# Convolution input product: channel blocks 2 to 6 by seven products, block 7 in full from tokens loaded a second time

## The chip, the cores and the metric

The kernel runs on one core of one Trainium2 chip. The metric is the device time of one execution in microseconds (us). The engines are TensorE (PE; its weight loads are PEld), VectorE (DVE), ScalarE (ACT), GpSimd (POOL) and SyncE (SP), which issues all of this kernel's transfers (DMA).

## What is computed

The reference is a decoder trunk of two layers in fp32, with 1024 tokens of 1024 channels. The first layer mixes tokens with a causal Conformer convolution, the second with sliding-window attention; each is followed by layer norm, an MLP with squared ReLU and a gated embedding. Only the convolution's start is touched here:

```python
def conformer_conv(x, w_in, b_in, w_dw, b_dw, ln_g, ln_b, w_out, b_out):
    h = x @ w_in + b_in                      # 1024 -> 2048
    a, gate = jnp.split(h, 2, axis=-1)
    h = a * jax.nn.sigmoid(gate)
    h = lax.conv_general_dilated(            # depthwise, 31 taps, causal
        h, w_dw[:, None, :], window_strides=(1,), padding=[(CONV_WIDTH - 1, 0)],
        dimension_numbers=("NWC", "WIO", "NWC"), feature_group_count=D_MODEL) + b_dw
    h = jax.nn.silu(layer_norm(h, ln_g, ln_b))
    return h @ w_out + b_out
```

## The kernel before

**Arithmetic.** Each fp32 operand is split into a high part and a remainder of a narrower type (fp32r): ScalarE casts (`xh`, `wh`), VectorE subtracts (`xl`, `wl`). A product is three matmuls, high by high, low by high and high by low (`mm3`, L663).

**Order.** The program is first recorded, and a list scheduler (`Recorder.schedule`, L318 to L454) then puts the instructions of all engines in an order, from a cost for each operation. For a DMA it takes the free time of the queue, and an amount that grows with the elements times partitions of the first operand (L446 to L449). Each engine runs its instructions in the order so made, and every instruction is recorded at line 466 (`issue`); so the profile's groups are told apart by tile names. `nc.later(n)` moves the due time of what is recorded under it, by `FORMS_BY` = 200 and `BACK_BY` = 300 for two parts of the convolution.

**Input products.** `conv` (L818 to L1129) works on eight channel blocks `c`; each has 128 channels of `a` and 128 of the gate, over two halves of 512 tokens. The tokens are held split as `xh`, `xl` in eight chunks of 128 input channels for each half. Blocks 0 to 2 (`c < ALONE`, `conv_in`) are computed in full: 2 outputs x 2 halves x 8 chunks x 3 = 96 matmuls of 128x512. Blocks 3 to 7 go by a Strassen-like scheme of seven products of half the depth (`conv_seven`): 7 x 4 x 3 = 84 matmuls. It needs differences of weight chunks (`pair_units`, L1224) and differences of token chunks, T1 to T4. `forms` (L854) makes T1 to T3: for each of four `k` it loads four token chunks from DRAM, three into `g` buffers (of which there are four) and one into an `E` buffer, takes the differences on VectorE, splits each into two buffers taken from other names (A, bo, v, B, X), and so frees the `g` buffers for the next `k`. `last_forms` (L871) splits T4 into the home of the tokens of the second half (`xT[0,1]`, tiles `xh`, `xl`), which so lose the plain tokens; it is called at the first block that goes by seven products.

**Exchange and taps.** `hand_over` (L836) splits a gated half (tile `zz`; `wh` for the last half of block 7) and stores it to DRAM (`scr`) in eight transfers. `taps` (L973) runs `LAG` = 6 steps behind: it loads `B` from `scr` with the tokens of a group on partitions, loads a band matrix `z` from `w_dw` (128x576, 288 KB; 64 of them in all), casts it into `E` on ScalarE over 128 partitions, puts the remainder of its upper 64 partitions beside it on VectorE, and does nine matmuls of 128x256 for each band, 72 for a block. The sums go to `g`, with the bias added by ScalarE, are transposed by TensorE (`tr<-ident,g`) and copied out: for blocks 0 to 6 (`c < KEPT`) as 128x512 to a `t` buffer and then to DRAM (`kept`). At block 7 the kept values come back into `X` and `A` in 64-element pieces, and block 7's own are copied beside them.

**After it.** `conv_ln` (L1053) is the layer norm: statistics on VectorE, scaling on POOL, transposes on TensorE, SiLU on ScalarE; `mix_out` is the output product. The embedding's products (`embed`, L1131; tiles `ps<-wh,wh`) need nothing from the convolution and are placed among the last taps and the layer norm.

Of the kernel before, what the change touches and what calls it, by code (L numbers as in the profile page):

```python
# [10 lines left out]
F32 = mybir.dt.float32  # L11
F32R = mybir.dt.float32r
# [3 lines left out]
P = 128  # L16
# [32 lines left out]
             ps=6, tr=2, sc=0, pv=0, mid=0)  # L49


ALONE = 3
KEPT = 7
FORMS_BY, BACK_BY = 200, 300
FORM_HOMES = ("A", 9), ("bo", 2), ("v", 1), ("B", 4), ("X", 8)
LATE = 100
# [66 lines left out]
class View:  # L123
# [30 lines left out]

    def to_broadcast(self, shape):
        return View(self.buf, np.broadcast_to(self.idx, shape[1:]), self.parts, self.steps + (("bro", shape),))

    def real(self):
        a = self.buf.tile
# [37 lines left out]
class Recorder:  # L197
# [120 lines left out]
    def schedule(self):  # L318
# [85 lines left out]
        while True:  # L404
            best = None
            for e in engs:
                while rdy[e] and rdy[e][0][2].end:
                    heapq.heappop(rdy[e])
                while fut[e] and fut[e][0][3].end:
                    heapq.heappop(fut[e])  # L410
                if rdy[e]:
                    t = free[e]
                elif fut[e]:
                    t = max(free[e], fut[e][0][0])
                else:
                    continue
                if best is None or t < best[0]:
                    best = (t, e)
            if best is None:
                break  # L420
            t, e = best
            while fut[e] and fut[e][0][0] <= t:
                r, p, i, o = heapq.heappop(fut[e])
                if not o.end:
                    heapq.heappush(rdy[e], (p, i, o))
            p, i, o = heapq.heappop(rdy[e])
            if WAIT and fut[e] and e != "tensor":
                r, p2, i2, o2 = fut[e][0]
                if not o2.end and r <= t + WAIT and p2 < p - 300:
                    heapq.heappush(rdy[e], (p, i, o))  # L430
                    heapq.heappop(fut[e])
                    t, o = r, o2
            if o.eng == "either":
                o.eng = e
                o.dur = self.cost(o, o.outv, o.allv)
            d = o.dur
            if e == "scalar" and o.name == "activation":
                k = TABLE.get(o.args[2].name if len(o.args) > 2 else "", 0)
                if k and k != table:
                    table = k  # L440
                    d += 1283.0
            if both(o):
                d += max(0.0, held["gpsimd" if e == "vector" else "vector"] - 50.0 - t)
                held[e] = t + d
            free[e] = t + d
            if e == "sync":  # L446
                v = o.allv[0]
                dma = max(dma, t + 1400.0) + v.n * v.parts / 75.0
                finish(o, max(dma, t + 2800.0))  # L449
            else:  # L450
                finish(o, t + d)
# [47 lines left out]
class Emit:  # L499
# [318 lines left out]
    def conv(self):  # L818
# [8 lines left out]
        ws.add(*[lambda k=k: self.prep(d["w_in"][0, k], range(4 * k, 4 * k + 4)) for k in range(2)])  # L827
        ws.pump()
        for c in range(1, 8):
            ws.add(*([d["w_in"][c, 0], d["w_in"][c, 1]] if c < ALONE else self.pair_units([d["w_in2"][c - ALONE, k] for k in range(2)])))  # L830
        nc.sync.dma_start(cc, d["cconst"])
        nc.sync.dma_start(self.ident, d["ident"])
        scr = {}
# [1 line left out]

        def hand_over(c, h, g):  # L836

            both = self.sb("wh" if (c, h) == (7, 0) else "zz", F32R, 2 * HT)
            self.split(g, both[:, 0:HT], both[:, HT : 2 * HT])
            for j in range(NG):  # L840
                if j % 2 == 0 and (c, j // 2) not in scr:
                    scr[c, j // 2] = nc.tile(f"scr{c}_{j // 2}", (P, 2 * U), F32, "DRAM")
                o = j % 2 * U + h * P
                cols = slice(o, o + P)
                dst = scr[c, j // 2].scatter(
                    lambda a, cols=cols: a.rearrange("(k p) u -> p k u", p=CG)[:, :, cols], CG, cols, 2 * PH
                )
                src = both.bitcast(F32)[j * CG : (j + 1) * CG, :].rearrange("p (k u) -> p k u", k=2 * PH)
                nc.sync.dma_start(dst, src)
# [84 lines left out]

        def conv_in(c):

            if c >= ALONE:
                yield from conv_seven(c)
                return
            us = ws.get(2)  # L940
            for h in (0, 1) if c == 0 else (1, 0):
                pp = [self.ps() for s in range(2)]

                def part(s, kb):
                    wh, wl = us[kb // 4]
                    o = (kb % 4) * 256 + (1 - s) * P
                    tr = [(wh[:, o : o + P], wl[:, o : o + P], *self.xs(kb, h * HT, HT))]
                    self.mm3(pp[s], tr, kb == 0, kb == KB - 1)

                if c == 0:  # L950
                    for kb in range(KB):
                        part(0, kb)
                        part(1, kb)
                    yield
                else:
                    for s in range(2):
                        for kb in range(KB):
                            part(s, kb)
                        if s == 0:
                            yield  # L960
                sg = self.sb("t")
                nc.scalar.activation(sg, pp[0], AF.Sigmoid, bias=bg[:, c : c + 1], scale=1.0)
                g = self.sb("t")
                nc.vector.scalar_tensor_tensor(
                    out=g, in0=pp[1], scalar=ba[:, c : c + 1], in1=sg, op0=ALU.add, op1=ALU.mult
                )
                hand_over(c, h, g)
                yield
            ws.done(2)
# [3 lines left out]
        def taps(c):  # L973
# [3 lines left out]
            for jj in range(2):  # L977
                pss = [self.ps() for k in range(2)]
                for j in range(2):
# [3 lines left out]
                    nc.sync.dma_start(G2[:, :, HIST : HIST + U], scr[c, 2 * jj + j].rearrange("p (k u) -> p k u", k=2))  # L983
                    exchange = nc.ops[-1]
                    for k in range(2):
                        w = nc.tile("z", (P, n))
                        nc.sync.dma_start(w, d["w_dw"][c, jj, 2 * j + k])
                        w = w.rearrange("p (m q) -> p m q", q=PH * CG)
                        e = bands[turn[0] % len(bands)]
                        turn[0] += 1  # L990
                        ev = e.rearrange("p (m o q) -> p m o q", o=2, q=PH * CG)
                        if e in fresh:
                            fresh.remove(e)
                            nc.gpsimd.memset(ev.bitcast(F32)[LOW, :, 1, :], 0.0)
                        nc.scalar.copy(ev[:, :, 0, :], w)
                        nc.vector.tensor_tensor(
                            out=ev[HIGH, :, 1, :], in0=w[HIGH], in1=ev[HIGH, :, 0, :].bitcast(F32), op=ALU.subtract
                        )
                        for i in range(SHIFTS):
                            o = k * LO + HIST - i  # L1000
                            nc.tensor.matmul(
                                pss[k][:, j * U : (j + 1) * U], e[:, i * P : (i + 1) * P], G[:, o : o + U],
                                start=i == 0, stop=i == SHIFTS - 1,
                            )
# [19 lines left out]
                        nc.tensor.transpose(pv[:, h, j], y[:, o : o + P], self.ident)  # L1024
                nc.slack = 0.0
                if c < KEPT:
                    s = self.sb("t")
                    (nc.scalar.copy if jj else nc.vector.tensor_copy)(s, pt)
                    nc.sync.dma_start(kept[:, (2 * c + jj) * HT : (2 * c + jj + 1) * HT], s)
                    yield  # L1030
                    continue
                if c == KEPT and jj == 0:
                    kv = kept.rearrange("p (c s u) -> p c s u", c=2 * KEPT, s=2 * PH)
                    for q in range(2):
                        m = min(8, 2 * KEPT - 8 * q)
                        for h in range(2):
                            for f in range(PH):
                                Z[h, f, q] = self.sb("XA"[q])
                                dst = Z[h, f, q][:, 0 : 64 * m].rearrange("p (c u) -> p c u", u=64)
                                with nc.later(BACK_BY):  # L1040
                                    nc.sync.dma_start(dst, kv[:, 8 * q : 8 * q + m, PH * h + f, :])
                for h in range(2):
                    for f in range(PH):
                        o = c % 4 * P + jj * 4 * CG
# [43 lines left out]
            forms()  # L1088
        more_bands()
        kept = self.dram("kept", 2 * KEPT * HT)  # L1090
        ins = (x for c in range(8) for x in conv_in(c))
        outs = (x for c in range(8) for x in taps(c))
        for n in range(32 + LAG):
# [902 lines left out]
def layout(a):  # L1996
# [12 lines left out]
    r["xT"] = c(x[phased].T.reshape(KB, P, T))  # L2009
    r["pT"] = c(np.stack([p[0][phased], p[1]]).transpose(0, 2, 1).reshape(2, 2, P, T))  # L2010
    wi = np.asarray(a["conv_w_in"])[0]
    r["w_in"] = c(wi.reshape(2, 4, P, 2, 8, P).transpose(4, 0, 2, 1, 3, 5).reshape(8, 2, P, 1024)[:ALONE])

    w2 = wi[:, np.concatenate([np.arange(D, 2 * D), np.arange(D)])].reshape(8, P, 2, 8, P)
    r["w_in2"] = c(w2.transpose(3, 2, 1, 0, 4).reshape(8, 2, P, 1024)[ALONE:])
# [12 lines left out]
    for q in range(CG):  # L2028
        band[:, :, :, :, q, :, q] = wt[:, :, :, :, q, :]
    band = band.reshape(8, 2, 4, P // 2, SHIFTS * PH * CG)  # L2030
    r["w_dw"] = c(np.concatenate([band, band], axis=3))

    bd = np.asarray(a["conv_b_dw"])[0].reshape(32, 2, CG).transpose(2, 1, 0).reshape(CG, 64)
    r["cconst"] = c(
# [45 lines left out]
```

## Time and profile before

| what | us |
|---|---|
| median of 3 runs | 2142.71 (2142.64 to 2142.78) |
| the profiled execution | 2142.3 |
| its span in the profile | 2140.5 |
| TensorE busy | 2116.5 |
| VectorE busy | 1757.5 |
| ScalarE busy | 1152.3 |
| GpSimd busy | 280.6 |

The convolution's input products and taps take about the first 260 us of the span, its layer norm and output product come after, the first MLP then runs to about 1000 us. A line of the page's groups reads "engine operation out<-in shape x count | busy us, mean ns | idle before, and what ended it"; a line of the timeline reads "start, duration, engine, operation, tiles, count [idle before it <- what ended it]". Matmuls overlap, so the mean duration of one (some 390 ns) is more than the distance from one to the next.

### The profile page before, as it was taken

Reading aid. Unit: us, or ns where it says so; the run is one execution under the profiler, and the core shown is the slowest. Engines: PE = TensorE matmul, PEld = TensorE weight load, DVE = VectorE, ACT = ScalarE, POOL = GpSimd, SP = SyncE. Lnnn points to the kernel's source line nnn. Section 1 sums busy time; section 2 is a strip of 40 time slices with the busy share of each in tenths; the row PEclk is TensorE's granted clock in tenths of the full one; section 3 lists DMA queues with packets and bytes.
Section 4 is the critical chain, followed back from the end, with each engine's and each line's share of the span. In section 5 each row is a group of like instructions: output and inputs, shape, how many; then the busy total and the mean of one; then the engine's idle time right before and its main releaser. Section 6 shows DMA issues by size and latency. Waiting matters only on the chain.

```text
span 2140.5 us, 29992 instructions
## 1 busy us (share of the span) xinstructions
PE 2116.5 (99%) x10008; PEld 1752.9 (82%) x10008; DVE 1757.5 (82%) x2854; ACT 1152.3 (54%) x2146; POOL 280.6 (13%) x495
## 2 busy tenths in 40 slices
PE   9999899999999999999999999999999999999999
PEld 7888778888888888888788888888888888888877
DVE  6866579988898788876986888689988988788688
ACT  5655554654544633335755888445445554333484
POOL 0000052200000000001320656240000000000042
PEclk9999999999999999999999999999999999999999
DMA  9877965867786756655487022665778795565726
GB/s 295 234 203 203 268 245 177 285 222 250 264 271 231 278 177 204 201 184 213 156 284 249 11 89 79 208 239 184 257 267 296 262 332 174 179 233 170 262 75 230
DMA packets 228939, 462.46 MB, mean 216 GB/s; under 512 B 38192, under 2 KB 64432, under 8 KB 228784
## 3 DMA queue, kind: packets, MB, share of 16 engines
q1 hardware_dynamic: 228784, 460.54, 65.1%
q8 instruction: 79, 1.29, 0.2%
q14 instruction: 76, 0.62, 0.1%
HBM read 312.34 MB, written 148.11 MB: 215 GB/s over the span
## 4 chain that ended last, share of the span: by engine, by line
PE 40%; DVE 5%; ACT 3%; DMA 2%; issue 1%; POOL 1%; SPq 0%; POOLq 0%; DVEq 0%; ACTq 0%
PE ps L466 31%; PE tr L466 9%; DVE xl L466 1%; DMA t<-proj 1%; ACT z L466 1%; DVE t L466 1%; POOL sm L466 1%; DVE z L466 1%; DVE sm L466 0%; DVE A L466 0%; DVE B L466 0%; ACT xh L466 0%; DMA raw<-in_w_kv_dram 0%; ACT t L466 0%; DMA raw<-gate_t 0%
## 5 line engine op out<-in xcount | busy, mean ns | idle before, releaser
L466 PE MATMUL ps<-xh,xl 128*128 128x512 f32 x636 | 247.6, 389 | 0.0
L466 PE MATMUL ps<-xh 128*128 128x512 f32 x636 | 247.6, 389 | 0.0
L466 PE MATMUL ps<-xl,xh 128*128 128x512 f32 x636 | 247.6, 389 | 0.0
L466 ACT CAST wh<-raw 128x1024 fp32r<-128x1024 f32 (+2 forms) x156 | 143.4, 923 | 134.7 <-PE ps L466 84.0
L466 POOL TENSOR_SCALAR sm<-sm 128x1 f32<-128x1 f32 x72 | 28.3, 397 | 1364.0 <-DVE E L466 612.0
L466 PE MATMUL ps<-xl,wh 128*128 128x512 f32 x508 | 198.7, 392 | 0.0
L466 PE MATMUL ps<-xh,wl 128*128 128x512 f32 x508 | 198.3, 391 | 0.0
L466 PE MATMUL ps<-xh,wh 128*128 128x512 f32 x508 | 196.1, 392 | 0.9 <-ACT xh L466 0.9
L466 PE MATMUL ps<-wh,xh 128*128 128x512 f32 (+1 forms) x404 | 159.2, 395 | 1.7 <-ACT zz L466 0.9
L466 PE MATMUL ps<-wh,xl 128*128 128x512 f32 (+1 forms) x404 | 160.4, 397 | 0.0
L466 PE MATMUL ps<-wl,xh 128*128 128x512 f32 (+1 forms) x404 | 159.3, 394 | 0.0
L466 ACT CAST wh<-g 128x512 fp32r<-128x512 f32 x128 | 76.4, 620 | 153.8 <-PE ps L466 73.7
L466 ACT CAST xh<-wh 128x1024 fp32r<-128x1024 f32 x76 | 79.7, 1049 | 118.0 <-PE tr L466 90.4
L466 PEld LDWEIGHTS ps<-xl,xh 128*128 128x128 f32 x636 | 119.4, 188 | 24.9
L466 PEld LDWEIGHTS ps<-xh,xl 128*128 128x128 f32 x636 | 119.4, 188 | 24.7
L466 PEld LDWEIGHTS ps<-xh 128*128 128x128 f32 x636 | 119.5, 188 | 24.6
L466 DVE TENSOR_TENSOR wl<-raw,wh 128x1024 fp32r<-128x1024 f32 (+1 forms) x100 | 100.0, 1001 | 35.5 <-ACT wh L466 35.1
L466 DVE TENSOR_TENSOR xl<-wh,xh 128x1024 fp32r<-128x1024 f32 x76 | 92.8, 1221 | 25.6 <-ACT xh L466 25.6
L466 PEld LDWEIGHTS ps<-xh,wh 128*128 128x128 f32 x508 | 95.4, 188 | 22.5 <-ACT xh L466 1.6
L466 PEld LDWEIGHTS ps<-xh,wl 128*128 128x128 f32 x508 | 95.5, 188 | 19.5
L466 PEld LDWEIGHTS ps<-xl,wh 128*128 128x128 f32 x508 | 95.4, 188 | 19.5 <-DVE xl L466 1.3
L466 DVE TENSOR_TENSOR wl<-g,wh 128x512 fp32r<-128x512 f32 x128 | 84.6, 686 | 26.8 <-ACT wh L466 26.8
(447 smaller groups left out, 5620.0 us busy)
## 6 DMA issues: line engine op xcount, KB each, us to landing
wh<-hid SPq DMA_DIRECT2D x78, 512.0 KB, 4.1
raw<-in_w_up_dram SPq DMA_DIRECT2D x61, 512.0 KB, 4.3
wl<-in_w_down_dram SPq DMA_DIRECT2D x58, 512.0 KB, 4.8
hid<-zz SPq DMA_DIRECT2D x96, 256.0 KB, 4.0
z<-in_w_dw_dram SPq DMA_DIRECT2D x64, 288.0 KB, 4.0
hid<-t SPq DMA_DIRECT2D x70, 256.0 KB, 3.0
raw<-hid SPq DMA_DIRECT2D x30, 512.0 KB, 3.7
B<-scr SPq DMA_DIRECT2D x32, 256.0 KB, 4.5
```

The source lines that it names most:

```text
L466: getattr(getattr(nc, o.eng), o.name)(*a, **k)
```

## The change

`ALONE` becomes 2, a new `LAST` is 7 and `KEPT` becomes 6. Blocks 2 to 6 go by seven products; blocks 0, 1 and 7 are computed in full. Since `last_forms` has overwritten the plain tokens of the second half's first four chunks, block 7 loads and splits these four chunks again, and starts with the half that has not been overwritten, and for the second half with the other four chunks. The number of matmuls stays at 10008.

Besides, the band matrices are loaded on 64 partitions (144 KB) and cast twice by ScalarE, once into each half of the partitions. The values kept in DRAM are ordered by half and phase, written in pieces of 128 elements and read back in one piece for each partition; block 6 is no longer kept but copied like block 7, which makes 16 more small copies. The scheduler's price of a DMA becomes the larger one of its operands' (9 ns for each contiguous piece and 0.0366 ns for each byte, over 16), which changes the order of instructions elsewhere too.

```diff
-ALONE = 3
-KEPT = 7
+ALONE = 2
+LAST = 7
+KEPT = 6
...
+    def transfer(self):
+
+        i = self.idx.ravel()
+        pieces = self.parts * (1 + int((np.diff(i) != 1).sum()))
+        return (9.0 * pieces + 0.0366 * 4 * i.size * self.parts) / 16
...
             if e == "sync":
-                v = o.allv[0]
-                dma = max(dma, t + 1400.0) + v.n * v.parts / 75.0
+                dma = max(dma, t + 1400.0) + max(v.transfer() for v in o.allv)
                 finish(o, max(dma, t + 2800.0))
...
-            ws.add(*([d["w_in"][c, 0], d["w_in"][c, 1]] if c < ALONE else self.pair_units([d["w_in2"][c - ALONE, k] for k in range(2)])))
+            ws.add(*([d["w_in"][c, 0], d["w_in"][c, 1]] if c < ALONE or c >= LAST else self.pair_units([d["w_in2"][c - ALONE, k] for k in range(2)])))
...
-            both = self.sb("wh" if (c, h) == (7, 0) else "zz", F32R, 2 * HT)
+            both = self.sb("wh" if (c, h) == (LAST, 1) else "zz", F32R, 2 * HT)
...
-            if c >= ALONE:
+            if ALONE <= c < LAST:
                 yield from conv_seven(c)
                 return
             us = ws.get(2)
-            for h in (0, 1) if c == 0 else (1, 0):
+            if c == LAST:
+                for kb in range(KB // 2):
+                    self.load_xT(1, kb)
+            for h in (0, 1) if c in (0, LAST) else (1, 0):
                 pp = [self.ps() for s in range(2)]
+                order = [(kb + KB // 2 * (h if c == LAST else 0)) % KB for kb in range(KB)]
...
-                        w = nc.tile("z", (P, n))
+                        w = nc.tile("z", (P // 2, n))
                         nc.sync.dma_start(w, d["w_dw"][c, jj, 2 * j + k])
...
-                        nc.scalar.copy(ev[:, :, 0, :], w)
+                        for rows in (HIGH, LOW):
+                            nc.scalar.copy(ev[rows, :, 0, :], w)
                         nc.vector.tensor_tensor(
-                            out=ev[HIGH, :, 1, :], in0=w[HIGH], in1=ev[HIGH, :, 0, :].bitcast(F32), op=ALU.subtract
+                            out=ev[HIGH, :, 1, :], in0=w, in1=ev[HIGH, :, 0, :].bitcast(F32), op=ALU.subtract
                         )
...
                 if c < KEPT:
-                    s = self.sb("t")
-                    (nc.scalar.copy if jj else nc.vector.tensor_copy)(s, pt)
-                    nc.sync.dma_start(kept[:, (2 * c + jj) * HT : (2 * c + jj + 1) * HT], s)
+                    for h in range(2):
+                        if jj == 0:
+                            wait[h] = self.sb("t")
+                        v = wait[h].rearrange("p (f j u) -> p f j u", f=PH, j=2)
+                        src = pt[:, h * 256 : (h + 1) * 256].rearrange("p (f u) -> p f u", f=PH)
+                        (nc.scalar.copy if h else nc.vector.tensor_copy)(v[:, :, jj, :], src)
+                        if jj:
+                            dst = kept.rearrange("p (s c u) -> p s c u", s=2 * PH, c=KEPT)
+                            nc.sync.dma_start(dst[:, PH * h : PH * h + PH, c, :], wait[h].rearrange("p (f u) -> p f u", f=PH))
                     yield
                     continue
                 if c == KEPT and jj == 0:
-                    kv = kept.rearrange("p (c s u) -> p c s u", c=2 * KEPT, s=2 * PH)
                     for q in range(2):
-                        m = min(8, 2 * KEPT - 8 * q)
+                        m = min(4, KEPT - 4 * q)
...
-                                    nc.sync.dma_start(dst, kv[:, 8 * q : 8 * q + m, PH * h + f, :])
+                                    nc.sync.dma_start(Z[h, f, q][:, 0 : P * m], kept[:, o : o + P * m])
...
+        wait = {}
```

More of the change, by code (lines that the diff above doesn't have):

```diff
@@ L947, in part @@
                     tr = [(wh[:, o : o + P], wl[:, o : o + P], *self.xs(kb, h * HT, HT))]
-                    self.mm3(pp[s], tr, kb == 0, kb == KB - 1)
+                    self.mm3(pp[s], tr, kb == order[0], kb == order[-1])
                 if c == 0:
@@ L956, in conv_in @@
                     for s in range(2):
-                        for kb in range(KB):
+                        for kb in order:
                             part(s, kb)
@@ L1038, in taps @@
                                 Z[h, f, q] = self.sb("XA"[q])
-                                dst = Z[h, f, q][:, 0 : 64 * m].rearrange("p (c u) -> p c u", u=64)
+                                o = ((PH * h + f) * KEPT + 4 * q) * P
                                 with nc.later(BACK_BY):
-                                    nc.sync.dma_start(dst, kv[:, 8 * q : 8 * q + m, PH * h + f, :])
+                                    nc.sync.dma_start(Z[h, f, q][:, 0 : P * m], kept[:, o : o + P * m])
                 for h in range(2):
@@ L2011, in layout @@
     wi = np.asarray(a["conv_w_in"])[0]
-    r["w_in"] = c(wi.reshape(2, 4, P, 2, 8, P).transpose(4, 0, 2, 1, 3, 5).reshape(8, 2, P, 1024)[:ALONE])
+    r["w_in"] = c(wi.reshape(2, 4, P, 2, 8, P).transpose(4, 0, 2, 1, 3, 5).reshape(8, 2, P, 1024))
     w2 = wi[:, np.concatenate([np.arange(D, 2 * D), np.arange(D)])].reshape(8, P, 2, 8, P)
@@ L2030, in layout @@
     band = band.reshape(8, 2, 4, P // 2, SHIFTS * PH * CG)
-    r["w_dw"] = c(np.concatenate([band, band], axis=3))
+    r["w_dw"] = c(band)
     bd = np.asarray(a["conv_b_dw"])[0].reshape(32, 2, CG).transpose(2, 1, 0).reshape(CG, 64)
```

## The prediction

> **What bounds the kernel now.** I read the page's busy shares first, then busy time by stretches, the waits of TensorE, its timeline around them, and last the queues that feed it. Of the page:
>
> ```profile
> span 2140.5 us, 29992 instructions
> PE 2116.5 (99%) x10008; PEld 1752.9 (82%) x10008; DVE 1757.5 (82%) x2854; ACT 1152.3 (54%) x2146; POOL 280.6 (13%) x495
> ```
>
> TensorE is the bound nearly everywhere, and the order of instructions shows 10008 matmuls in both kernels. So the change cannot remove matmul time; it can only remove or make idle time on TensorE. Where that is, the busy time by stretches shows (us, busy and count of PE, PEld, DVE, ACT, POOL, granted clock, DMA share, GB/s):
>
> ```profile
> 50.00:225.00 175.00, 174.43 (x997) 152.55 (x996) 125.67 (x188) 102.84 (x183) 4.75 (x31) 1.00 0.77 221
> 225.00:310.00 85.00, 76.20 (x423) 63.20 (x422) 56.74 (x108) 50.05 (x97) 27.83 (x33) 0.98 0.89 278
> 310.00:1000.00 690.00, 688.97 (x3067) 569.09 (x3066) 586.68 (x849) 320.08 (x480) 26.12 (x27) 1.00 0.69 230
> ```
>
> The steady convolution (50 to 225 us) loses 0.6 us and the first MLP 1.0 us; the end of the convolution with its layer norm (225 to 310 us) loses 8.8. That stretch is what can be won. What TensorE waits for in it (total us, times, longest), and where (start, duration, idle before in brackets):
>
> ```profile
> PE ps L466 <- DVE E L466: 2.1, 2, 1.1
> PE ps L466 <- POOL X L466: 1.8, 1, 1.8
> PE ps L466 <- DVE g L466: 1.7, 2, 1.2
> PE ps L466 <- ACT xh L466: 1.6, 1, 1.6
> PE tr L466 <- POOL X L466: 1.0, 3, 0.4
> PE ps L466 <- POOL A L466: 0.5, 1, 0.5
> ```
> ```profile
> 55.16 2.31 PE L466 MATMUL ps<-B,E 128*128 128x256 f32 x18
> ...
> 228.74 4.46 PE L466 MATMUL ps<-B,E 128*128 128x256 f32 x36
> 234.30 1.34 PE L466 MATMUL ps<-B,E 128*128 128x256 f32 x9 [1.09 <-DVE E L466]
> 236.67 2.12 PE L466 MATMUL ps<-B,E 128*128 128x256 f32 x9 [1.03 <-DVE E L466]
> ...
> 252.07 8.77 PE L466 MATMUL ps<-B,E 128*128 128x256 f32 x72
> 260.68 0.40 PE L466 MATMUL ps<-wh,wl 128*128 128x512 f32 x1
> ```
>
> The last input product ends at 228.74, the last tap at 260.68: 31.9 us. The 72 taps took 260.68 - 252.07 = 8.6 us, 0.12 each. A 128x512 matmul costs 0.227 (16.32 us for 72, in the chain of waits):
>
> ```profile
> 1502.43 16.32 PE ps L466 x72
> ```
> ```profile
> L466 PE MATMUL ps<-B,E 128*128 128x256 f32 x126 | 16.7, 292 | 2.1 <-DVE E L466 2.1
> L466 PE MATMUL ps<-wh,wh 128*128 128x512 f32 x12 | 5.0, 415 | 3.3 <-DVE g L466 1.7 <-ACT xh L466 1.6
> ```
>
> By these groups of the tail (228.7 to 260.8), it holds 126 taps (15.1 us), 37 matmuls of 128x512 (the row shows 12 of them; 8.4 us) and 8 transposes (0.9, some 0.11 each by the same pitch per column): 24.4 us of work, so 7.5 lost. 2.1 + 3.3 = 5.4 are the named waits; the rest is mostly a lower clock (the granted clock is the third column from the end):
>
> ```profile
> 236.00:238.00 2.00, 1.33 (x7) 1.33 (x8) 1.31 (x2) 0.68 (x2) 0.00 (x0) 0.72 0.99 263
> 238.00:240.00 2.00, 1.64 (x8) 1.24 (x7) 1.19 (x2) 1.72 (x4) 0.00 (x0) 0.50 0.98 351
> 240.00:242.00 2.00, 1.19 (x5) 1.01 (x6) 1.97 (x4) 1.97 (x4) 0.00 (x0) 0.92 0.99 228
> ```
>
> After two waits of a microsecond the clock ran at half for some 3.4 us: 0.28 x 2 + 0.50 x 2 + 0.08 x 2 = 1.7 us lost.
>
> **The change, part by part.** A profiled run of before took 2142.3 us; the median of the runs is 2142.71, 0.4 above. I sum against 2142.3 and add 0.4.
>
> *Token forms a block earlier (ALONE 3 to 2).* Block 2 by seven products needs twelve token forms, made in four rounds through four "g" buffers: load four chunks (three of them into g buffers), subtract them on VectorE, cast on ScalarE, subtract again, free. They are now needed a block sooner, and the scheduler puts them earlier into VectorE's order. The rows of before (VectorE):
>
> ```profile
> 35.68 0.75 DVE L466 SCALAR_TENSOR_TENSOR t<-ps,cst,t 128x512 f32<-128x512 f32 x1 [3.66 <-ACT t L466]
> ...
> 57.13 0.75 DVE L466 TENSOR_TENSOR E<-z,E 64x576 fp32r<-64x576 f32 x1 [0.19 <-ACT E L466]
> ...
> 61.85 0.68 DVE L466 TENSOR_TENSOR g<-g,g 128x512 f32<-128x512 f32 x1
> 62.45 0.68 DVE L466 TENSOR_TENSOR zz<-t,zz 128x512 fp32r<-128x512 f32 x1
> ```
> ```profile
> DMA to landing us min/median/max: 2.7/3.5/5.3
> ```
>
> The second row is the band subtraction that the second 18 taps wait for; the fourth-round subtraction (61.85) stands after it. The last two starts are 0.60 apart: the price of an instruction in this queue. The landing row is that of the g buffers from 30 to 66 us. In the changed order the same band subtractions (bands 3 and 4) stand at places 76 and 77 of VectorE, fourteen places behind the fourth round's second subtraction (62), where before they stood ahead of it (60 and 61, against 62 and 65). TensorE comes to these taps two matmuls earlier in its row of products but after the first 18 taps: 55.16 - 2 x 0.227 + 18 x 0.12 = 56.9. The rounds: the second can start about 36.3 (right behind the row at 35.68, its loads being issued at the same place as before), and each is one landing and six instructions, 3.5 + 3.6 = 7.1 us, so the third runs at 43.4 and the fourth at 50.5; its second subtraction, four instructions on, at 52.9. Fourteen more instructions, 8.4, give 61.3, and the subtraction itself 0.7: 62.0. TensorE waits 62.0 - 56.9 = 5.1 us, and its queue is in order: all later products wait with it. With three landings at 2.7 or 5.3 the wait is 2.7 or 10.5; if the first subtractions are not late, 0. I take the median. Such a wait brings the half clock, 1.7 as above (0 if there is no wait). Two weight pairs of block 2 also free their "raw" buffers later, as a difference of theirs stands in the same queue: 0 to 2, I take 0.8 as it overlaps most of the wait. Together +7.6, between 0 and +14.2.
>
> *The end of the input products (block 7 in full, last half handed over alone).* In the new order 54 taps (6.5 us), 4 transposes (0.4) and two embedding matmuls (0.5) stand between the last product and the last 72 taps: 7.3 us of cover. Against it runs the exchange. Its rows (ScalarE; SyncE; then, from 60 to 215 us, the landings of the bands' input and of B):
>
> ```profile
> 34.96 0.69 ACT L466 ACTIVATE t<-ps,cst 128x512 f32<-128x512 f32 x1 [3.76 <-PE ps L466]
> ...
> 38.75 0.62 ACT L466 CAST zz<-t 128x512 fp32r<-128x512 f32 x1
> ```
>
> ```profile
> 236.34 4.31 SPq L466 DMA_DIRECT2D scr<-zz  x8
> ...
> 241.22 3.71 SPq L466 DMA_DIRECT2D scr<-wh  x8
> ...
> 246.89 1.89 SPq L466 DMA_DIRECT2D B<-scr  x3
> ```
> ```profile
> DMA to landing us min/median/max: 2.7/3.7/6.4
> ```
> ```profile
> DMA to landing us min/median/max: 3.1/3.8/5.9
> ```
>
> Gate 0.7, product 0.75, cast 0.6, subtraction 0.7, eight stores 3.7, one issue of B 0.6, landing 3.8: 10.8. So 3.5 us stay uncovered, with 1.0 of lower clock (under the 1.7, as it is one wait and not two), and 0.4 where ScalarE, which has 20 band casts, 14 activations and 10 copies (some 21 us) beside 20 to 23 of TensorE, is late. 4.9 in place of 7.5: -2.6. The bounds: 0 (every wait comes back) and -7.5.
>
> *Band input on 64 partitions, cast twice.* The 64 loads are halved in bytes, so the bands' input lands sooner and stands less in SyncE's way; this is in the term above (the 2.1 of DVE E, and the slack for B). ScalarE gets 64 casts more:
>
> ```profile
> L466 ACT CAST E<-z 128x576 fp32r<-128x576 f32 x46 | 30.5, 665 | 4.7 <-PE tr L466 2.3 <-DMA z<-in_w_dw_dram 1.8 <-PE ps L466 0.3
> ```
>
> 46 x 0.665 = 30.5 us more in the steady part: ScalarE there goes from 102.84 to 133 of 175. It stays under TensorE, so it costs little; I put +0.5 (0 to +3, a tenth of the added time) for it and for the four token chunks of block 7 loaded again, which 48 matmuls (10.9 us) of its first half hide. If that cover went, a landing (3.7) would show, which the +3 about holds.
>
> [...] No row here has a load onto 64 partitions. [...]
>
> *Kept blocks through DRAM.* Written in 512-byte pieces and read back contiguously, where the read was in 256-byte pieces; the reads now come a block sooner:
>
> ```profile
> L466 SPq DMA_DIRECT2D X<-kept x8: 384/532/3234, 217.0 to 230.2; - x8
> ```
>
> Single issues took up to 3.2 us on SyncE, ahead of the bands' loads; that is part of the tail's 2.1. Sixteen more small copies of block 6 go beside TensorE: nothing.
>
> *Layer norm.* 78 embedding matmuls in place of 62 are left behind the last tap: 16 x 0.227 = 3.6 us of filler against POOL's waits of 1.8 + 1.0 + 0.5 = 3.3. Not all filler falls in the right place: -2.3, between 0 and -3.3.
>
> *The scheduler's new price of a DMA* reorders all the rest. Matmuls stay, the MLPs' orders are nearly the same: 0, with 3 either way.
>
> Sum: +7.6 - 2.6 + 0.5 - 2.3 = +3.2; profiled 2145.5, median 2145.9.
>
> **The rivals.**
> 1. The forms come at the upper bound: landings of 5.3, the weights' 2.0 in full. +14.2 in place of +7.6: 2152.5. For it: four loads of w_dw, the stores and B stand in the same SyncE queue. Against: the median landing.
> 2. Faster: the forms come in time. If the fourth round's second subtraction starts by 56.9 - 0.7 - 8.4 = 47.8 in place of 52.9, TensorE doesn't wait: 2145.9 - 7.6 = 2138.3. For it: the reordered queue may find each load landed before its turn, and rounds overlap with four buffers. Against: in before the third round's loads were issued behind the stores. The sign turns where the early loss falls under 4.4 us.
> 3. The part meant for the tail does nothing there: bands and exchange end as late as they did, 7.5 lost again, for the 64-partition input lands no sooner. 2145.9 + 2.6 = 2148.5. For it: landing rows of g, 3.5, and bands, 3.7, hardly differ with 256 and 288 KB, so bytes may not set a landing. Against: SyncE is held by pieces, of which there are fewer.
>
> **How the numbers follow.** Forecast 0.40 (its own range 2140 to 2151), rival one 0.22, two 0.23, three 0.15. What a measurement of this kernel tells from no change is about 0.2%, 2138.4 to 2147.0. Same: 0.26 from the forecast, 0.06 from two, 0.05 from three: 0.37. Faster: 0.17 from two (its tail may reach its bound of -7.5), 0.03 from the forecast: 0.20. Slower: 0.11 + 0.22 + 0.10 = 0.43. The range holds rivals one and two with a little beyond each: 2136 to 2153.
>
> **What the changed profile would show.** For the early step: a wait of TensorE on DVE E of some 5 us near 57 us with a clock of 0.50 behind it; none there says rival two, over 9 says one. For the tail: from the last product to the last tap 24 us of work and under 5 lost, the wait on DVE E gone and one on B in its place; if DVE E's 2.1 stands, rival three. For the layer norm: POOL's waits under 1.5. The prediction is wrong altogether if a stretch after 310 us loses over 3 us more than before, from the reordering.

## The result, and the profile after

| kernel | median, us | runs | ratio to before (95% interval) |
|---|---|---|---|
| before | 2142.68 | 4 | |
| changed | 2194.21 (2191.18 to 2195.40) | 4 | 1.0238 (1.0221 to 1.0256) |

The change costs 51.5 us; the prediction had +3.2 and a range up to 2153.0. The profiled execution of the changed kernel took 2191.2 us, 1.7 above its span. From its page:

```profile
span 2189.5 us, 30103 instructions
PE 2135.0 (98%) x10008; PEld 1760.8 (80%) x10008; DVE 1763.7 (81%) x2866; ACT 1197.8 (55%) x2227; POOL 290.8 (13%) x500
```

The 10008 matmuls are all there, so the 49 us of longer span are idle or slow time of TensorE. By stretches (the convolution shifted by some 10 us; columns as in the prediction):

```profile
50.00:235.00 185.00, 170.13 (x929) 147.47 (x929) 128.67 (x196) 133.30 (x233) 4.59 (x29) 0.95 0.70 179
235.00:320.00 85.00, 78.42 (x448) 67.04 (x447) 55.26 (x108) 63.18 (x124) 25.38 (x33) 0.96 0.74 235
320.00:1020.00 700.00, 692.40 (x3063) 569.03 (x3062) 584.56 (x837) 320.30 (x481) 29.51 (x29) 1.00 0.67 223
```

The steady convolution now loses 14.9 us (0.6 before), and the first MLP, whose instructions the diff touches only through the scheduler's price, 7.6 (1.0 before). Where the time comes in is read best from when the n-th matmul (counted from 0) starts in either trace. TensorE runs 10008 of them in both, in much the same order, so the delay against before can be followed (us, worked out from the start times; where taps and products change places, about a microsecond of it is only order):

| matmul | 250 | 1000 | 1250 | 1500 | 3500 | 5250 | 5500 | 8500 | 10000 |
|---|---|---|---|---|---|---|---|---|---|
| before starts it at | 59.1 | 190.9 | 234.3 | 285.7 | 732.6 | 1120.7 | 1173.8 | 1800.8 | 2134.8 |
| delay, changed | 10.2 | 13.1 | 20.7 | 19.4 | 30.4 | 31.9 | 40.1 | 47.0 | 49.3 |

Ten of them come before 70 us, some 9 until the layer norm, and 30 behind it: 11 from matmul 1500 to 3500, most of the first MLP, 8 at the start of the attention (5250 to 5500), and 9 from there to 10000, most of them in the second MLP.

**Near 60 us.** The timelines of TensorE and of VectorE in the changed kernel:

```profile
58.46 0.39 PE L472 MATMUL ps<-xh,wh 128*128 128x512 f32 x1
66.38 3.96 PE L472 MATMUL ps<-B,E 128*128 128x256 f32 x17 [7.53 <-issue]
```
```profile
57.05 0.69 DVE L472 TENSOR_TENSOR g<-g,g 128x512 f32<-128x512 f32 x1 [1.01 <-DMA g<-in_xT_dram]
...
64.94 0.68 DVE L472 TENSOR_TENSOR zz<-t,zz 128x512 fp32r<-128x512 f32 x1
65.54 1.41 DVE L472 TENSOR_TENSOR E<-z,E 64x576 fp32r<-64x576 f32 x2
```

This has the form and the place of the forecast wait. The second subtraction of the fourth round starts at 57.05, having waited for its load; the fourteenth instruction behind it, the subtraction of the band that these taps need, starts at 65.54; the taps start as it ends. The profile puts the wait down to "issue"; that it is this subtraction is inferred from the times, as the last cast of a band on ScalarE starts at 58.42, 8 us earlier. The runs below show that the split alone does not make this wait. From 66 to 70 us the granted clock was 0.50:

```profile
66.00:70.00 4.00, 3.62 (x17) 3.65 (x18) 3.38 (x5) 2.32 (x4) 0.00 (x0) 0.50 0.72 124
```

**Ahead of the tail and in it.** TensorE's longest wait after that stands still among the input products: a transpose that needs `g`, the taps' sums with bias. In the timelines of TensorE, ScalarE and VectorE:

```profile
224.95 1.12 PE L472 MATMUL tr<-ident,g 128*128 128x128 f32 x4 [5.57 <-DVE g L472]
```
```profile
218.34 0.69 ACT L472 ACTIVATE t<-ps,cst 128x512 f32<-128x512 f32 x1 [1.59 <-DMA kept<-t]
...
221.37 2.06 ACT L472 CAST E<-z 64x576 fp32r<-64x576 f32 x3
223.34 0.82 ACT L472 ACTIVATE g<-ps,cst 64x256 f32<-64x256 f32 x2
```
```profile
224.20 0.69 DVE L472 TENSOR_TENSOR g<-g,ps 64x512 f32<-64x512 f32 x1
```

The last two of the four bias activations ran at 223.34, behind three of the new band casts (2.06 us), and earlier ScalarE had stood 1.59 us for a `t` buffer that a store to `kept` still held. VectorE's sum and then the transposes followed. The last input product starts at 250.38 us, and the last tap ends at 278.6. From 200 to 330 us TensorE's waits were:

```profile
PE tr L472 <- DVE g L472: 5.6, 1, 5.6
PE ps L472 <- DVE g L472: 2.1, 1, 2.1
PE tr L472 <- POOL X L472: 1.9, 1, 1.9
PE ps L472 <- DMA B<-scr: 1.1, 1, 1.1
PE ps L472 <- DVE E L472: 1.1, 1, 1.1
PE ps L472 <- ACT E L472: 0.3, 1, 0.3
```

The first is the one above. The wait on POOL comes after the last tap, and the other four, 4.6 us together, stand between the last product and the last tap.

**In the first MLP** VectorE waits for stores out of `zz`. The groups of `zz<-t,zz` from 310 to 1060 us of before and, further down, from 330 to 1075 us of the changed kernel (busy, mean ns, then idle before and its end):

```profile
L466 DVE TENSOR_TENSOR zz<-t,zz 128x512 f32<-128x512 f32 x16 | 11.0, 687 | 3.6 <-DMA hid<-zz 3.4
```
```profile
L472 DVE TENSOR_TENSOR zz<-t,zz 128x512 f32<-128x512 f32 x16 | 11.1, 692 | 25.9 <-DMA hid<-zz 24.0 <-issue 1.9
```

The stores themselves land hardly later, median 3.7 us before and 3.9 after, over the tile `hid`:

```profile
DMA to landing us min/median/max: 2.0/3.7/8.8
```
```profile
DMA to landing us min/median/max: 2.0/3.9/8.1
```

So slower transfers are not the reason (the landing row covers all the transfers of `hid`, stores and loads); the instructions stand sooner behind them. VectorE's 24 us are not all TensorE's: it loses 7.6 in the first MLP.

### The profile page after: what moved, and what is told of

The parts are those of the page before. It is cut to its first block, busy times and chain, and to the rows that moved or that the text cites. A ratio compares the mean times of both kernels' runs of the same rounds, so it can differ in the third digit from the quotient of the medians.

```text
span 2189.5 us, 30103 instructions
## 1 busy us (share of the span) xinstructions
PE 2135.0 (98%) x10008; PEld 1760.8 (80%) x10008; DVE 1763.7 (81%) x2866; ACT 1197.8 (55%) x2227; POOL 290.8 (13%) x500
## 4 chain that ended last, share of the span: by engine, by line
PE 35%; DMA 6%; DVE 5%; ACT 4%; issue 1%; POOL 0%; SPq 0%; ACTq 0%; DVEq 0%; POOLq 0%
PE ps L472 28%; PE tr L472 7%; ACT z L472 1%; DVE xl L472 1%; DMA raw<-gate_t 1%; DMA hid<-zz 1%; DMA raw<-in_w_q_dram 1%; DMA w_q<-X 1%; ACT wh L472 1%; DVE t L472 1%; DVE wl L472 1%; DMA form<-t 1%; DVE z L472 0%; ACT xh L472 0%; ACT t L472 0%
## 5 line engine op out<-in xcount | busy, mean ns | idle before, releaser
L472 PE MATMUL ps<-xl,xh 128*128 128x512 f32 x654 | 254.5, 389 | 0.9 <-DVE xl L472 0.9
L472 PE MATMUL ps<-xh,xl 128*128 128x512 f32 x654 | 254.4, 389 | 0.0
L472 PE MATMUL ps<-xh 128*128 128x512 f32 x654 | 254.4, 389 | 0.0
L472 PE MATMUL ps<-wh,xh 128*128 128x512 f32 x504 | 201.4, 400 | 1.8 <-DVE t L472 1.5
L472 PE MATMUL ps<-wl,xh 128*128 128x512 f32 x504 | 200.7, 398 | 1.3 <-DMA wl<-gate_low_t 1.3
L472 PE MATMUL ps<-wh,xl 128*128 128x512 f32 x504 | 200.8, 398 | 0.0
L472 PEld LDWEIGHTS ps<-wh,xh 128*128 128x128 f32 x504 | 95.4, 189 | 21.2 <-DVE t L472 2.4
L472 PEld LDWEIGHTS ps<-wl,xh 128*128 128x128 f32 x504 | 95.3, 189 | 18.9 <-DMA wl<-gate_low_t 2.2
```

What stands on the lines that cost most here:

```text
L472: getattr(getattr(nc, o.eng), o.name)(*a, **k)
```

## The experiments

Every kernel was measured beside runs of the kernel before on the same chip, whose medians were 2141.9 to 2143.2. The delay at a matmul is worked out as above, from one profiled execution.

**What the parts cost: the price, and the split.** The first two runs add the new price of a DMA to the kernel before, and take it out of the changed one:

```diff
-                v = o.allv[0]
-                dma = max(dma, t + 1400.0) + v.n * v.parts / 75.0
+                dma = max(dma, t + 1400.0) + max(v.transfer() for v in o.allv)
```

> The kernel before with only the scheduler's new price of a DMA. Theory A (the new price is too low, transfers are believed to land sooner than they do, and what is ordered by it waits, all over the program): some 25 to 35 us slower, 2168 to 2178, with TensorE's waits spread over the convolution, the first MLP and the start of the attention as in the changed kernel. Theory B (the split of the blocks, 2 to 6 by seven and 7 in full, is what costs; the price only reorders): 2143, 3 either way.

> The changed kernel with the old price of a DMA; block split, bands on 64 partitions and the layout of the kept blocks stay. Theory A: the 28 us lost behind 325 us are gone and the early wait of 7.5 us too, 2140 to 2155. Theory B: still 2180 to 2195.

Measured: the price alone 2176.79, ratio 1.0161 (1.0132 to 1.0191), +34; the changed kernel without it 2158.24, ratio 1.0075 (1.0045 to 1.0104), 36 less than with it. Either way the price is two thirds of the loss. The second run is 3 us above what theory A gave, so something else costs too. In the run with the price alone the delay is 6.7 at matmul 1000, 18.9 at 3500, 28.6 at 5500 and 35.8 at 10000; without the price it stays at 13 to 15 from matmul 1500 on. With the price alone, VectorE's row of `zz<-t,zz` from 310 to 1060 us is that of the changed kernel again:

```profile
L471 DVE TENSOR_TENSOR zz<-t,zz 128x512 f32<-128x512 f32 x16 | 11.1, 692 | 25.9 <-DMA hid<-zz 25.9
```

Counted from the start of the program, these sixteen instructions stand two to six places earlier in VectorE's order than before. In the changed kernel with the old price, the wait for the stores is 1.9. What TensorE waits for at the start of the attention was not followed back. One place in the first MLP of the price-alone run shows how it comes about, in the timeline of SyncE, the landing of the one load of `raw` in that stretch (685 to 702 us), and the timelines of VectorE, ScalarE and TensorE:

```profile
692.30 0.45 SPq L471 DMA_DIRECT2D raw<-in_w_up_dram  x1
```
```profile
DMA to landing us min/median/max: 7.2/7.2/7.2
```
```profile
699.53 0.69 DVE L471 TENSOR_TENSOR g<-raw 128x512 f32<-128x512 f32 x1 [3.61 <-DMA raw<-in_w_up_dram]
700.90 0.69 DVE L471 TENSOR_TENSOR zz<-t,zz 128x512 f32<-128x512 f32 x1 [0.67 <-DMA hid<-zz]
701.51 0.69 DVE L471 TENSOR_TENSOR g<-g,raw 128x512 f32<-128x512 f32 x1
```
```profile
700.32 0.62 ACT L471 CAST wh<-g 128x512 fp32r<-128x512 f32 x1 [5.77 <-DVE g L471]
702.23 0.62 ACT L471 CAST wh<-g 128x512 fp32r<-128x512 f32 x1 [1.29 <-DVE g L471]
702.76 0.58 ACT L471 COPY t<-ps 128x512 f32<-128x512 f32 x1
```
```profile
703.39 0.73 PE L471 MATMUL ps<-A,wh 128*128 128x512 f32 x2 [1.83 <-ACT t L471]
```

The order puts VectorE's difference of weights, by all appearances, where the plan has the load landed; the plan's own times are not in the trace. It landed 7.2 us after its issue, other transfers being on their way with it (from 690 to 701 us the queue's transfers took 77.9% of the DMA engines' time); VectorE stands 3.61, then again for a store; ScalarE's cast stands 5.77 behind VectorE; and the copy `t<-ps`, which has nothing to do with either, stands behind the casts in ScalarE's order and starts at 702.76. TensorE waits 1.83 us for it.

The next two give the split alone, and the changed kernel with the price raised (`1.3 * max(v.transfer() ...)`).

> The kernel before with only the block split (2 to 6 by seven products, block 7 in full from tokens loaded again, block 6 not kept); price, bands and layout as before. If the early wait comes from the forms being needed a block sooner, as the prediction had it, TensorE waits 5 us or more near 57 us and the time is 2148 to 2158. If it comes from the price's order, no such wait, and 2140 to 2145. Theory B: 2180 or more.

> The changed kernel with the new price times 1.3, by which a whole 128x512 transfer costs the scheduler the same 0.87 us as by the old price. If only the level of the price was too low (theory A), within 5 us of the changed kernel with the old price. If the form of the price (a count of pieces, the larger operand) is what costs, as slow as the changed kernel, 2185 to 2195.

Measured: the split alone 2147.45 in 7 runs, ratio 1.0025 (1.0012 to 1.0037). Its delay is -1.1 at matmul 250, 7.4 at 500 and then 6 to 8 to the end: the loss lies between about 58 and 85 us, near the place that the step with the token forms named. But it is not the forecast wait. TensorE's waits from 20 to 130 us of the split alone are short ones:

```profile
PE ps L467 <- ACT E L467: 1.8, 1, 1.8
PE ps L467 <- ACT t L467: 1.1, 1, 1.1
PE ps L467 <- DVE E L467: 0.9, 1, 0.9
PE tr L467 <- DVE g L467: 0.6, 2, 0.4
PE ps L467 <- issue: 0.2, 1, 0.2
```

The longest comes at 62 us, and after it the granted clock is 0.50 for 3.4 us. In VectorE's order the subtractions of bands 3 and 4 stand ahead of the fourth round's second subtraction (places 60 and 61 against 69), and not fourteen places behind it. The changed kernel with the old price has no wait of 7.5 us either: its longest there is 2.7. So neither sign of the expectation (a wait of 5 us, 2148 to 2158) is met, if narrowly in time, and the one long wait of the changed kernel needs the split and the new price together. The changed kernel with the price raised took 2155.95, ratio 1.0065 (1.0042 to 1.0088), the same as with the old price within 3 us. Raising the level alone takes the price's loss away.

**Bands and layout.** Bands on 64 partitions cast twice, and the layout of the kept blocks, each alone in the kernel before, and each with the split:

> The kernel before with only the band matrices loaded on 64 partitions and cast twice. The step as the prediction took it (half the bytes land sooner, the casts hide): 2140 to 2143, and the bands' landing under its 3.7 us. If ScalarE's 64 further casts come out on the path (theory C): 2146 to 2151, with TensorE waiting for ACT and DVE E in the steady convolution. If half the partitions land no sooner: the landing stays near 3.7.

> The kernel before with only the new layout of the kept blocks. If reading back in one piece frees the queue at the tail: 2139 to 2143. If the two t buffers held from one half-step of a block to the next make ScalarE and VectorE wait for the stores of kept (theory D): 2145 to 2152, with ACT t waiting for DMA kept<-t.

> Block split and bands on 64 partitions, old price, old layout of the kept blocks. The split alone took 2147.5, split, bands and layout 2158.2. Theory C (the casts): 2154 to 2159. Theory D (the t buffers): 2146 to 2149.

> Block split and the new layout of the kept blocks, old price, bands on 128 partitions. Theory C: 2146 to 2149. Theory D: 2154 to 2159. Where both cost: 2150 to 2154.

Measured: bands alone 2152.88, ratio 1.0050 (1.0027 to 1.0073); layout alone 2144.23, ratio 1.0007 (0.9995 to 1.0018); split and bands 2160.65, ratio 1.0087 (1.0057 to 1.0116); split and layout 2147.60, ratio 1.0028 (1.0017 to 1.0039). So the bands cost 11 to 13 us in either company, under two more than theory C allowed, and the layout none that can be told. The busy time of the bands-alone run from 50 to 225 us, and the bands' landing from 60 to 215 us:

```profile
50.00:225.00 175.00, 170.13 (x966) 147.62 (x966) 121.43 (x182) 132.57 (x227) 4.08 (x28) 1.00 0.66 174
```
```profile
DMA to landing us min/median/max: 2.5/3.2/6.4
```

ScalarE goes from 102.84 to 132.57 us, the 133 that the prediction worked out, and yet TensorE gets 966 matmuls done there and not 997, and loses 4.9 us in place of 0.6. Theory C's sign is there only in part: TensorE's waits of this stretch are 2.2 us for `B` from the exchange, 1.4 for `g`, 0.8 for ACT `t` and 0.4 for DVE `E`; after 225 us it waits 3.8 for ACT `E` too. The bands land a little sooner in this run, 3.2 in place of 3.7, beside less traffic (a DMA share of 0.66 in place of 0.77). In the changed kernel, from 60 to 235 us, they do not:

```profile
DMA to landing us min/median/max: 2.6/3.8/7.0
```

So whether half the bytes on 64 partitions land sooner in themselves is not shown: the two landings, 3.2 and 3.8 in place of 3.7, are medians over issue and transfer together, each beside other traffic.

Are the casts the cause? One run loads on 128 partitions as before and only casts in two halves; another loads on 64 and puts the added cast on GpSimd.

```diff
-                        nc.scalar.copy(ev[:, :, 0, :], w)
+                        for rows in (HIGH, LOW):
+                            nc.scalar.copy(ev[rows, :, 0, :], w[rows])
```
```diff
-                        for rows in (HIGH, LOW):
-                            nc.scalar.copy(ev[rows, :, 0, :], w)
+                        nc.scalar.copy(ev[HIGH, :, 0, :], w)
+                        nc.gpsimd.tensor_copy(ev[LOW, :, 0, :], w)
```

> The kernel before with the band matrices loaded on 128 partitions as before, but cast in two instructions of 64 partitions each. Bands on 64 partitions took 2152.9, 10 to 11 more than before. If the 64 further casts on ScalarE are what costs (theory C): 2150 to 2155. If the load onto 64 partitions costs: 2141 to 2144.

> The kernel before with bands on 64 partitions, the added cast on GpSimd in place of ScalarE. If only ScalarE's casts cost (theory C): 2141 to 2145. If the load onto 64 partitions costs the 4 us that the two casts alone leave open: 2145 to 2149. If GpSimd's cast is late itself: over 2150, with VectorE or TensorE waiting for POOL E.

Measured: two casts from 128 partitions 2149.27 (2145.26 to 2153.87, 8 runs), ratio 1.0033 (1.0020 to 1.0045); the cast on GpSimd 2152.40, ratio 1.0042 (1.0022 to 1.0061). The first is below theory C's 2150 to 2155, though above what was expected if only the load cost. Taking the casts off ScalarE gives nothing back. On GpSimd the added casts took 907 ns in the mean of the 62 from 50 to 310 us (670 in the median of the 45 from 60 to 215 us, the longest 2601), and GpSimd too waits for TensorE to release `E` and for the loads:

```profile
L466 POOL CAST E<-z 64x576 fp32r<-64x576 f32 x62 | 55.9, 907 | 139.7 <-PE ps L466 78.7 <-DMA z<-in_w_dw_dram 47.1 <-issue 12.6
```

TensorE waits 5.5 us for DVE `E` and 7.6 for `B` from the exchange there, and its weight loads wait 7.9 for GpSimd's `E`: the cast on GpSimd comes late itself. So this run doesn't clear the load, and the cause within the bands stays open.

**The forms.** The split without its early part (`ALONE` 3, `LAST` 7, `KEPT` 6, 12 matmuls more), and the split with the forms' due time moved up:

```diff
-FORMS_BY, BACK_BY = 200, 300
+FORMS_BY, BACK_BY = 0, 300
```

> The split without its early part: blocks 0 to 2 and 7 in full, 3 to 6 by seven products; price, bands and layout as before. It has 12 more matmuls of 128x512, 12 x 0.227 = 2.7 us. If the split's loss near 60 us comes from the forms being needed a block sooner, that loss (8.5 us up to matmul 500) is gone, and the time is 2142 plus 2.7 less what the tail gains, 2141 to 2145. If it comes from elsewhere, 2148 to 2152.

> The split (2147.5) with the due time of the token forms moved up by 200 (FORMS_BY 0 in place of 200). If what costs is that they come too late in VectorE's order for block 2: 2143 to 2146, the wait on the bands near 62 us smaller. If there is too much work ahead of block 2 whatever the order: 2147 to 2152.

Measured: 2144.48, ratio 1.0001 (0.9990 to 1.0012), and 2143.77, ratio 1.0006 (0.9995 to 1.0017). With `ALONE` 3 the delay at matmul 500 is 0.5 where the split had 7.4; with the forms moved up it is 2.7, and -0.2 by matmul 1500. Both met their expectation, and both point to the same cause of the split's loss: the forms being late for block 2.

**The level of the price.** Raising it by half in the kernel before:

```diff
-                dma = max(dma, t + 1400.0) + v.n * v.parts / 75.0
+                dma = max(dma, t + 1400.0) + v.n * v.parts / 50.0
```

> The kernel before with the old price of a DMA raised by half (elements times partitions over 50 in place of 75). If a price that is too low costs and one that is too high does not (theory A as it stands): 2140 to 2146. If any other price loses the order that was settled with the old one, as with the new price: 2150 or more.

Measured: 2328.84, ratio 1.0865 (1.0833 to 1.0896). Theory A as it stood fell here: too dear is worse than too cheap. The plan adds all transfers up in one line. 462.46 MB are 115.6 million elements; at 50 for each ns the line takes 2.31 ms, longer than the 2.14 ms of the kernel, so the plan is paced by a queue that is not full: on the page of before its transfers took 65% of the engines' time.

```profile
q1 hardware_dynamic: 228784, 460.54, 65.1%
```

At 75 the line is 1.54 ms. That the plan waits for this line is argued from its sum; the waits that it leaves are shown in TensorE's list:

```profile
PE ps L466 <- ACT t L466: 40.3, 11, 15.1
PE ps L466 <- ACT xh L466: 35.2, 7, 11.6
```

Then the new price's level with the old form, and the old price's level with the new form: the old form over 97.5 (0.67 us for a 128x512, as the new price has it), and the new form times 1.3 in the kernel before.

> The kernel before with the old form of the price, lowered by 1.3 (over 97.5 in place of 75), so that a 128x512 transfer costs the scheduler the 0.67 us of the new price. If the level is what costs: 2165 to 2185, with VectorE waiting for stores as in the run with the new price alone. If the form: 2141 to 2150.

> The kernel before with the new form of the price, raised by 1.3 to the old level. If the level is what costs: 2141 to 2150. If the form: 2165 to 2185.

Measured: 2188.87, ratio 1.0218 (1.0188 to 1.0248), and 2156.27, ratio 1.0067 (1.0044 to 1.0089). So the low level costs by either form, 46 us with the old and 34 with the new. The first is 4 us beyond what was expected for the level, the second 6 us, so up to 13 us come with the form or with the order that it makes. The last two runs show how much of such a rest can be a new order alone, with the old price over 77 and over 73:

> The kernel before with the old price lowered by 2.6 per cent (over 77 in place of 75). If a new order by itself costs little, 2141 to 2146. If the order of before was a lucky one among its neighbours, 2148 to 2158; then what the bands and the raised price cost is within what any new order costs, and no mechanism of theirs is shown by their times alone.

> The same, raised by 2.7 per cent (over 73). Little by itself: 2141 to 2146. A lucky order before: 2148 to 2158.

Measured: 2149.06, ratio 1.0036 (1.0008 to 1.0065), and 2143.42, ratio 1.0003 (0.9992 to 1.0014). A new order costs 0 to 6 us by itself, and the first of the two falls where the expectation had a lucky order before. The price's 34 is far beyond that. The split's 4.7 is not, by its time alone; its place in the trace and the two runs on the forms show it. The 6 us of the two casts are no more than what the order made by dividing by 77 costs, so no mechanism of theirs is shown by the time, and of the bands' 11 about half may be order.

**What is left of the change.** Split and layout, old price, bands on 128 partitions, forms moved up:

> The change without its two dear parts: block split and layout of the kept blocks, old price, bands on 128 partitions, and the forms' due time moved up (FORMS_BY 0). The split with FORMS_BY 0 took 2143.8 and the layout costs 0 to 2: 2142 to 2147. If the layout's faster reading back pays once the forms are in time: 2138 to 2142.

Measured: 2143.64, ratio 1.0008 (0.9996 to 1.0020): no gain over the kernel before. No run beats it beyond its interval. Taken alone, price, bands, split and layout cost 34.1, 11.0, 4.7 and 2.4 us, 52.2 together against the 51.5 of the change; as an order alone can move the time by 6, that they add up so closely may be luck.

## Why the prediction was wrong

- **The scheduler's new price of a DMA, "0, with 3 either way": this is the step that failed.** It measured +34 alone and 36 within the change. I had found the order of the MLPs nearly the same and took that for no cost. But a few places in an engine's order were enough: with `zz<-t,zz` two to six places earlier, stores that land as before held VectorE 25.9 us in place of 3.4, and 24.0 in the changed kernel. The new price puts a 128x512 transfer at 0.67 us, the old one at 0.87, and both can be worked out from the diff; the sign at least could have been read from that, as a plan that believes transfers done sooner leaves less room behind each. The prediction named a sign of being wrong altogether, a stretch after 310 us that loses over 3 us more from the reordering: the first MLP loses 7.6 in place of 1.0.
- **Bands cast twice, +0.5 (0 to +3): far too small, and the second step that failed.** Without the new price the kernel takes 2158.2, still beyond the range. The bands cost 11 us with the kernel before, 13 with the split. The added busy time was right to a microsecond, and the sentence "It stays under TensorE, so it costs little" was wrong. ScalarE's share is an average: at 221 us of the changed kernel three casts (2.06 us) stand ahead of bias activations that VectorE's sum needs, and TensorE then waits 5.57 us for that sum. How much of the 11 us comes in this way, from the load or from a new order is not settled.
- **Token forms, +7.6: near in place and size, but only half right in mechanism.** In the changed kernel the wait was 7.5 us in place of 5.1, since the fourth round's second subtraction came at 57.05 and not 52.9, and TensorE was itself 1.8 later; the clock of 0.50 followed. In all 10.2 by matmul 250. The rule "over 9 says rival one" is not met by the wait. But the fourteen places between that subtraction and the bands come with the new price: the split alone has several waits of under 2 us and a delay of 7.4 by matmul 500, so that the size agrees with the forecast is in part luck. That late forms are behind it, the two runs on the forms show.
- **The tail, -2.6: not found.** From the last input product to the last tap the changed kernel takes 28 us. Its 126 taps, 15 matmuls of 128x512 and 12 transposes are 19.8 us at the prediction's costs, so 8.2 are lost, as many as before: counted by the same start times, before has 35 of the larger matmuls in its tail where the prediction's rows, which reach over its edges, had 37, and loses 8.1 and not 7.5. The split alone loses 9.0. The exchange was forecast well: the wait for `B` ends at 262.27, 11.7 us after the last product, against 10.8. What the sum lacked is the wait of 2.1 us for `g`, the taps' sums, and the granted clock of 0.50 from 260 to 266 us, around its end; of DVE `E`'s 2.1 half stands. Rival three had this outcome, a tail in which nothing is won; its reason, the load that lands no sooner, fits the landing of 3.8 us but is not shown to be the cause. Fewer pieces held SyncE less in one case only: the issue of a read from `kept` into `X` took 0.39 us (median) in place of 0.53, that of a band's load 0.48 in place of 0.37.
- **Layer norm, -2.3: right.** From the last tap to matmul 1600 TensorE loses 3.0 us in the changed kernel and 2.0 in the split alone, against 5.3 before (spans less the same costs): 2.3 and 3.3 won. The waits on POOL are 1.9, not under 1.5 but less than the 3.3 of before.
- **Kept blocks, nothing: right**, 2144.23 with an interval that holds no change.

Rivals: none had the price as its mechanism, and rival one, at 2152.5, was the nearest in time only.

## What to carry to other kernels

Where a planner sets the order of every engine, a change of one cost in it can touch every stage, not only the one that the diff is about (here 30 of the 49 us came behind the layer norm); price such an edit first, by what it makes the plan believe to be ready sooner or later than the trace shows, and expect a change from the new order by itself, 0 to 6 us here where the cost moved by 3%. Here a cost that was too low made engines wait for transfers (VectorE 25.9 us in place of 3.4 for the stores out of `zz`, with the price alone); that one too high made the plan itself wait for a queue that isn't full is argued from its sum. An engine with time to spare can still hold the fullest one, when its work stands ahead of something short that the other needs: in the changed kernel ScalarE was busy 133.30 of the 185 us from 50 to 235, and three of its casts at 221 us still stood ahead of the activations behind which TensorE, 98% busy over the whole, waited 5.57 us.

## What the runs showed that was not expected

- Taking 2.6% off the price of a transfer cost 6 us, adding 2.7% nothing that can be told, and 50% more cost 186 us: 1.0036, 1.0003 and 1.0865 of the time before.
- The 64x576 casts on GpSimd took 907 ns in the mean. On ScalarE such a cast took as long for 64 partitions as for 128, 672 ns median in the changed kernel against a mean of 665 in the row of before, so halving the partitions did not shorten it here:

```profile
L472 ACT CAST E<-z x92: 655/672/682, 69.1 to 230.8; 64x576 fp32r<-64x576 f32 x92
```
